# Gate and up of sixteen column tiles of FFN 1 by Strassen, and the SSM preparation rewritten and spread differently

## The chip, the cores and the metric

One NeuronCore of a Trainium2 chip runs the whole kernel in one launch. The metric is the device time of one execution in microseconds (us). The engines are named as in the profile: PE (TensorE, matmuls; PEld is its weight loads), DVE (VectorE), ACT (ScalarE), POOL (GpSimd) and SP (SyncE, which here only issues DMAs). Each engine takes its instructions strictly in the order of the program's queue for it, and waits at an instruction whose operand or buffer is not ready.

## The reference

One decoder layer on x of 512 tokens by 1024 channels, all float32: a half-step SwiGLU, then an SSM and a sliding-window attention side by side, then a second half-step SwiGLU and a last norm.

```python
h = rms_norm(x, ffn1_norm)
x = x + 0.5 * ((silu(h @ w_gate) * (h @ w_up)) @ w_down)      # FFN 1, d_ff = 2816
h = rms_norm(x, mix_norm)
u, q, k, v = split(h @ w_in, [512, 1024, 1152])
y_ssm  = s5_mixer(u, ...)                    # 32 groups of 16 channels, 64 complex states each
y_attn = swa_sink_attention(rope(q), rope(k), v, sinks)       # 8 heads of 64, window 128
x = x + concat(rms_norm(y_ssm), rms_norm(y_attn)) @ w_out
h = rms_norm(x, ffn2_norm)
x = x + 0.5 * swiglu(h, ...)                 # FFN 2, the same shapes
return rms_norm(x, final_norm)

# s5_mixer, from the parameters alone:
lam_bar = exp((A_re + i A_im) * exp(log_dt))
B_bar   = ((lam_bar - 1) / lam) * (B_re + i B_im)
# state[t] = lam_bar * state[t-1] + B_bar @ u[t];  y = Re(C @ state) + D * u, then gelu and a gate
```

## The kernel before

**Matmuls.** Channels lie on the 128 partitions, tokens on the 512 columns. To keep float32 accuracy every operand is split into a high and a low part (`hi`, `lo` of activations, `whi`, `wlo` of weights), and `mm3` (L182 to L184) makes each product of three matmuls: hi x whi, lo x whi, hi x wlo. A weight block comes by DMA into `wraw` (SP's queue), ACT casts it to `whi`, DVE subtracts to get `wlo`; `wraw`, `whi` and `wlo` have three buffers each, so an engine that prepares a block waits until the block three before it has been read.

**FFN.** d_ff is 22 column tiles of 128. A classical tile is two PSUM tiles `gu` (gate and up), each 8 input blocks x 3 matmuls of 512 columns. Tiles come in groups (`FGROUPS`); after each group its activations (`activate`: `g`, `s`, `u`, `a`, then `hi` and `lo`) go into the eight `dn` columns m = 0 to 7 of the down projection, whose results are added to x (`x<-dn,x`). The norm's factor R is not applied to h ahead of the first matmuls but to their results.

**Strassen in FFN 2.** Tiles 6 to 21 of FFN 2 go in eight pairs through `pairs` already: a pair of column tiles and the two halves of tokens and input channels form 2x2 blocks, and gate and up take 7 products each of 4 input blocks x 3 matmuls of 256 columns (PSUM `gua`, `gub`, `guc`). `quarters` prepares the operands on the activation side: h with gain and R applied, sums of its quarters on POOL (`qe`, `q`, `qd`), and their hi and lo parts in `xq`, `xh`, `xr`, `xu`, `xx`. `pair_weights` loads each pair's weights (`wraw`, 512 KB, and two `wb`, 256 KB each, from `wgs2`) and adds four sums on POOL (`s0` to `s3`): `s0` from the two `wb`, `s1` from `s0` and `wraw`. Product n=2 reads `s1`. A product's weights are cast and subtracted two products ahead (`AHEAD`).

**SSM preparation.** `prep_steps` computes from the parameters: the small values (`scr`, 128x32), B_bar and its seven products with powers of lam_bar, one after the other in steps of 256 columns (`chain_b`: 6 POOL operations each, results in `aB`), transposes of these (`tV` on PE, copied to `matV`), the short kernel of the SSM (`qp`, 32 small matmuls with `cbr` and `ncbi`, evaluated to `qs` and written to `dz` in DRAM), the phases `rho`, `ec`, `es` of the state scan by doubling, and C times the powers (`chain_c`: 45 POOL operations of 512 columns, `matC`). The steps are a list; `ffn` takes one from it behind each `gu` tile and each `dn` column of FFN 1, so they spread over all of FFN 1.

**Mixing.** The strings of `ORDER` set in which order the steps of SSM and attention are written: U the projections, K, k and Q, q keys and queries, P the state scan, Y the SSM's output, S and E the scores. The order in which each engine finally gets its instructions comes from a scheduler that works from this program order and the buffers.

## Time and profile before

| | |
|---|---|
| runs | 935.74, 935.38, 925.63 us (median 935.38) |
| profiled execution | span 925.4 us (no time of its own is given; the nearest run is the one of 925.63) |
| granted PE clock, mean | 0.994 |
| PE busy | 907.5 us, 98% |
| DVE, ACT, POOL busy | 624.0, 369.2, 314.9 us |
| FFN 1, mixing, FFN 2 | about 5 to 388, 388 to 559, 559 to 925 us |

A line of a group reads: line of the kernel, engine, operation, result<-operands, shape, how often | busy us in all, mean ns of one | idle us of its engine just before, and what ended that. A line of the timeline reads: start us, duration us, engine, line, operation. PE's ends are modelled, so consecutive matmuls overlap in it.

### The profile page before, as it was taken

To read this page: it belongs to the slowest core of one execution; us is meant where nothing else is said; L and a number is where in the kernel's file an instruction comes from. 1 tells how busy PE (TensorE), PEld (TensorE's weight loads), DVE (VectorE), ACT (ScalarE), POOL (GpSimd) and SP (SyncE) were. 2 spreads that over 40 slices of the span, in tenths; PEclk is the share of its full clock that TensorE was granted. 3 is DMA by queue.
4 is the path that set the end of the run, shared out by engine and by line. 5 is a ranking of instruction groups with operands and counts; after the bars stand their busy time and mean duration, and the time that the engine had idled before them with its cause. 6 is when DMAs were issued, how large, how long until landed. Compare 5 with 4: busy or idle time off the path is not lost.

```text
span 925.4 us, 13303 instructions
## 1 busy us (share of the span) xinstructions
PE 907.5 (98%) x5036; PEld 772.9 (84%) x5036; DVE 624.0 (67%) x1167; ACT 369.2 (40%) x660; POOL 314.9 (34%) x272
## 2 busy tenths in 40 slices
PE   9999999999999999999979999999999999999996
PEld 6887888888888888888868887888899889988995
DVE  7886444474464443958896787697588459855966
ACT  7142233222232322622487433543355335532553
POOL 0009902179950000501231063180553055404502
PEclk9999999999999999999989999999999999999998
DMA  7332423243213321547201122215421442135112
GB/s 244 125 92 53 153 91 103 64 133 121 84 57 112 114 76 56 164 149 186 78 1 46 46 79 104 91 36 157 150 86 35 134 156 87 35 110 180 47 47 91
DMA packets 37503, 91.92 MB, mean 99 GB/s; under 512 B 8032, under 2 KB 10304, under 8 KB 37184
## 3 DMA queue, kind: packets, MB, share of 16 engines
q1 hardware_dynamic: 37008, 90.54, 31.3%
q8 instruction: 39, 0.64, 0.3%
q10 hardware_dynamic: 432, 0.55, 0.2%
q14 instruction: 24, 0.20, 0.1%
HBM read 87.44 MB, written 3.64 MB: 98 GB/s over the span
## 4 chain that ended last, share of the span: by engine, by line
PE 91%; DVE 5%; ACT 2%; issue 1%; DMA 1%; SPq 0%; DVEq 0%; ACTq 0%
PE gu L182 11%; PE gu L183 11%; PE gu L184 11%; PE dn L182 9%; PE dn L183 8%; PE dn L184 8%; PE gua L184 3%; PE gua L183 3%; PE gua L182 3%; PE guc L184 2%; PE guc L182 2%; PE guc L183 2%; PE ow L182 2%; PE ow L183 2%; PE ow L184 2%; PE pt L1037 1%
## 5 line engine op out<-in xcount | busy, mean ns | idle before, releaser
L154 ACT CAST whi<-wraw 128x1024 fp32r<-128x1024 f32 (+4 forms) x134 | 122.6, 921 | 307.6 <-PE gu L183 118.9
L173 DVE TENSOR_TENSOR wlo<-wraw,whi 128x1024 fp32r<-128x1024 f32 (+4 forms) x133 | 155.4, 1173 | 42.6 <-ACT whi L154 42.5
L182 PE MATMUL gu<-hi,whi 128*128 128x512 f32 x448 | 178.9, 402 | 1.5 <-ACT hi L195 1.4
L183 PE MATMUL gu<-lo,whi 128*128 128x512 f32 x448 | 176.7, 395 | 0.1
L184 PE MATMUL gu<-hi,wlo 128*128 128x512 f32 x448 | 176.3, 395 | 0.0
L183 PE MATMUL dn<-lo,whi 128*128 128x512 f32 (+1 forms) x336 | 130.1, 389 | 0.0
L182 PE MATMUL dn<-hi,whi 128*128 128x512 f32 (+1 forms) x336 | 130.1, 392 | 0.0
L184 PE MATMUL dn<-hi,wlo 128*128 128x512 f32 (+1 forms) x336 | 128.9, 389 | 0.0
L182 PEld LDWEIGHTS gu<-hi,whi 128*128 128x128 f32 x448 | 84.4, 189 | 21.8 <-ACT hi L195 2.3
L184 PEld LDWEIGHTS gu<-hi,wlo 128*128 128x128 f32 x448 | 84.3, 188 | 19.7
L183 PEld LDWEIGHTS gu<-lo,whi 128*128 128x128 f32 x448 | 84.5, 189 | 19.2 <-DVE lo L197 1.0
L182 PEld LDWEIGHTS dn<-hi,whi 128*128 128x128 f32 x336 | 63.3, 188 | 14.9 <-ACT whi L154 1.1
L184 PEld LDWEIGHTS dn<-hi,wlo 128*128 128x128 f32 x336 | 63.2, 188 | 14.2
L183 PEld LDWEIGHTS dn<-lo,whi 128*128 128x128 f32 x336 | 63.3, 188 | 13.6
L269 POOL TENSOR_TENSOR sq<-sq 128x512 f32<-128x512 f32 x17 | 25.1, 1476 | 139.9 <-ACT sq L265 137.2
L537 DVE TENSOR_TENSOR wlo<-s,whi 128x512 fp32r<-128x512 f32 x64 | 55.2, 904 | 12.2 <-ACT whi L536 12.0
L502 POOL TENSOR_TENSOR s<-s,wraw 128x512 f32<-128x512 f32 x32 | 50.4, 1576 | 33.9 <-DMA wraw<-wgs 32.9
L502 POOL TENSOR_TENSOR s<-wb 128x512 f32<-128x512 f32 x16 | 23.6, 1474 | 112.3 <-DMA wb<-wgs 91.4
L345 DVE TENSOR_TENSOR u<-gu,R 128x512 f32<-128x512 f32 x28 | 19.2, 685 | 48.2 <-PE gu L184 48.2
L412 DVE SCALAR_TENSOR_TENSOR x<-dn,x 128x512 f32<-128x512 f32 x32 | 21.7, 685 | 42.7 <-PE dn L184 42.7
L536 ACT CAST whi<-s 128x512 fp32r<-128x512 f32 x64 | 36.5, 618 | 30.4 <-issue 9.3
L428 DVE SCALAR_TENSOR_TENSOR x<-dn,x 128x512 f32<-128x512 f32 x24 | 16.5, 690 | 46.2 <-PE dn L184 46.2
(371 smaller groups left out, 2030.1 us busy)
## 6 DMA issues: line engine op xcount, KB each, us to landing
wraw<-wgu SPq DMA_DIRECT2D x54, 512.0 KB, 3.4
wraw<-wd SPq DMA_DIRECT2D x40, 384.0 KB, 3.2
wb<-wgs SPq DMA_DIRECT2D x32, 256.0 KB, 5.2
wraw<-wgs SPq DMA_DIRECT2D x16, 512.0 KB, 3.7
wraw<-wd SPq DMA_DIRECT2D x16, 320.0 KB, 2.9
...
x<-xT SPq DMA_DIRECT2D x8, 256.0 KB, 5.1
...
```

The costliest lines, as they stand in the source:

```text
L154: (e.copy if e is self.nc.scalar else e.tensor_copy)(out, x)
L173: self.eng("lo" + key).tensor_tensor(lo, raw, hi.bitcast(F32), op=ALU.subtract)
L182: mm(out, wh, xh, start=start, stop=False, **kw)
L183: mm(out, wh, xl, start=False, stop=False, **kw)
L184: mm(out, wl, xh, start=False, stop=stop, **kw)
L269: (eng or b.nc.gpsimd).tensor_tensor(self.acc, self.acc, sq, op=ALU.add)
L345: nc.vector.tensor_tensor(u, pu, self.R, op=ALU.mult)
L412: nc.vector.scalar_tensor_tensor(self.x[m], ps, 0.5, self.x[m], op0=ALU.mult, op1=ALU.add)
L428: self.nc.vector.scalar_tensor_tensor(self.x[m], ps, 0.5, self.x[m], op0=ALU.mult, op1=ALU.add)
L502: add = lambda o, x, y: nc.gpsimd.tensor_tensor(o, x, y, op=ALU.add)
L536: self.chained("A", lambda: A.copy(hi[:, c], w))
L537: self.chained("V", lambda: V.tensor_tensor(lo[:, c], w, hi[:, c].bitcast(F32), op=ALU.subtract))
```

## The change

FFN 1 gets what FFN 2 has: its groups become (0,6), (6,12), (12,18), (18,22), and tiles 6 to 21 go through `pairs(1, ...)`. `quarters(1)` prepares the operands during tiles 4 and 5 and the first down; its buffers are taken from tiles that the SSM preparation used (`rce`, `u4`, `big`) and from the pool of 512-column tiles, which grows from 43 to 49.

The SSM preparation is rewritten. A table of the powers of lam_bar (`pw`, `ppw`) replaces the step-by-step chains: `b_powers` makes `aB` with 24 operations of 512 columns, half on POOL and half on DVE, and `c_powers` makes `matC` with 24, likewise. The exponential of `er`, the B_bar factor and the copies go from DVE to POOL. Everything up to `qp` and `dz` is done by the end of the first down (`early`); `rho`, `ec`, `es`, the doublings and `matC` are done in the last down and in the mixing stage (`late`, the new `B` entries of `ORDER`). The loads of `s_prm`, `sB`, `cbr`, `cbi` and `sD` go from SP's queue to ACT's.

```diff
-FGROUPS = {1: ((0, 6), (6, 12), (12, 17), (17, 22)), 2: ((0, 6), (6, 12), (12, 18), (18, 22))}
+FGROUPS = {1: ((0, 6), (6, 12), (12, 18), (18, 22)), 2: ((0, 6), (6, 12), (12, 18), (18, 22))}
-ORDER = ("R0 U0 U1 R1 u0 u1 l0 U2 U3 u2 u3 l1 K0 P0 K1 L0 k0 P1 C0 L1 t0 C1 Y0 C2 C3 q0 q2 Q0 q1 Q2 q3 Y1 S0 "
+ORDER = ("R0 U0 B3 U1 B1 R1 u0 u1 l0 U2 B1 U3 B1 u2 u3 l1 K0 B1 P0 K1 L0 k0 B2 P1 C0 B2 L1 t0 B2 C1 Y0 C2 C3 q0 q2 Q0 q1 Q2 q3 Y1 S0 "
...
-        self.m2p = ctx.enter_context(tc.tile_pool(name="m2p", bufs=43))
+        self.m2p = ctx.enter_context(tc.tile_pool(name="m2p", bufs=49))
...
+    def ffn1(self):
+        xg, wgu, wd = self.xg, self.d["wgu1"], self.d["wd1"]
+        early, self.late = self.prep_steps()
+        prep = self.quarters(1)
+        take = lambda q, n: [q.pop(0) for _ in range(n)]
+        slots = [take(early, n) for n in (1, 1, 2, 2, 2, 3, 2, 0)]
+        scale = prep.pop(0)
+        slots += [take(prep, 1), take(prep, 1), take(early, 4) + take(prep, 2), take(early, 4) + take(prep, 1),
+                  take(early, 1) + take(prep, 1), [], [], take(early, 1) + take(prep, 1)]
...
+        scale()
+        self.down(wd, 0, NCL, acts, background)
+        for f0, f1 in FGROUPS[1][1:]:
+            acts = self.pairs(1, range((f0 - NCL) // 2, (f1 - NCL) // 2))
+            if f1 < NF:
+                self.down(wd, f0, f1, acts, lambda m: None)
+        self.prenorm(self.g_mix)
...
-        def chain_b(s):
+        def b_powers(r, q4):
             def f():
...
+                e = (G, V)[r]
+                qs = slice(q4 * 4, q4 * 4 + 4)
...
+                t = [S.m2(name="tB").rearrange("p (q c s) -> p q c s", q=4, s=T) for _ in range(2)]
+                tt(t[0], x[r], y[0], ALU.mult, e)
+                tt(t[1], x[1 - r], y[1], ALU.mult, e)
+                tt(aB[:, r, qs], t[0], t[1], (ALU.subtract, ALU.add)[r], e)
             return f
...
-            nc.sync.dma_start(cr, d["sCbd"][:, 0])
-            nc.sync.dma_start(ci, d["sCbd"][:, 1])
-            nc.sync.dma_start(dd, d["sD"])
+            for t, src in ((cr, d["sCbd"][:, 0]), (ci, d["sCbd"][:, 1]), (dd, d["sD"])):
+                nc.scalar.dma_start(t, src)
...
+        def c_powers(g8, e):
             def f():
...
+                tt(t[0], x[0], y[0], ALU.mult, e)
+                tt(t[1], x[1], y[1], ALU.mult, e)
+                tt(S.matC[:, gs], t[0], t[1], ALU.add, e)
             return f
...
+        for g8 in range(8):
+            late.append(c_powers(g8, (G, V)[g8 % 2]))
```

At the start of FFN 1, ACT's queue held before: `hi` of the last two x tiles, the first `whi` of tile 1, the eight squares `sq`, six more `whi`; now it holds the eight squares and the load of `sB` ahead of the first `whi` of tile 1. Ahead of the activation of tile 5, DVE's queue now holds all twelve DVE operations of `b_powers` (`tB`, `aB`). Three places in rows:

PE, at the first `qp` matmul. Before, it stood in the second group's `gu` tiles:

```order
L183 MATMUL gu<-lo,whi 128x512
L184 MATMUL gu<-hi,wlo 128x512
L854 MATMUL qp<-cbr,aB 128x32
L182 MATMUL gu<-hi,whi 128x512
L183 MATMUL gu<-lo,whi 128x512
```

Now it stands in the first down, between the last matmul of column m=5 and the first of m=6:

```order
L182 MATMUL dn<-hi,whi 128x512
L183 MATMUL dn<-lo,whi 128x512
L184 MATMUL dn<-hi,wlo 128x512
L909 MATMUL qp<-cbr,aB 128x32
L182 MATMUL dn<-hi,whi 128x512
```

ACT at the same place, now (`xr`, `xm`, `xu` are parts of the quarter-operands, made from POOL's sums `q`, `qe`, `qd`; `whi` of L559 is the first product of the first pair, of L154 a down column's):

```order
L478 ACTIVATE xr<-qe 128x512 x2
L475 CAST xm<-h 128x256 x2
L154 CAST whi<-wraw 128x768
L475 CAST xm<-h 128x256 x2
L475 CAST xu<-qd 128x512
L475 CAST xm<-h 128x256 x2
L478 ACTIVATE xr<-q_1015 128x512
L475 CAST xm<-h 128x256 x2
L559 CAST whi<-wraw 128x512 x2
L903 DMA cbr<-sCbd 128x512
L903 DMA cbi<-sCbd 128x512
```

The load of `cbr` has moved behind casts that wait for POOL and for a weight buffer. Before, SP issued it among the weight loads of the second group:

```order
L171 DMA wraw<-wgu 128x1024 x12
L171 DMA wraw<-wd 128x768
L846 DMA cbr<-sCbd 128x512
L847 DMA cbi<-sCbd 128x512
L848 DMA sD<-sD 128x512
L171 DMA wraw<-wd 128x768 x5
L872 DMA dz<-qs 16x8x256
L869 DMA dz<-zero 16x7x256 x2
L872 DMA dz<-qs 16x8x256
```

SP now, from the loads of the first down on (`wb` of the first row of two are gate's of the first pair, of the second up's):

```order
L171 DMA wraw<-wd 128x768 x8
L521 DMA wraw<-wgs 128x1024 x3
L524 DMA wb<-wgs 128x512 x2
L927 DMA dz<-qs 16x8x256
L924 DMA dz<-zero 16x7x256 x2
L927 DMA dz<-qs 16x8x256
L524 DMA wb<-wgs 128x512 x2
L521 DMA wraw<-wgs 128x1024 x2
```

The four `dz` transfers, which stood among the last weight loads of a down, now stand between the weights of gate and up of one pair. DVE in the mixing stage, at the end of the state scan (`wr`, `ro`, `S`), before; `kL` belongs to the keys, and `ra`, `rb`, `q` rotate the queries:

```order
L1172 TENSOR_TENSOR ro_3825<-wi,ec 128x512
L1184 TENSOR_TENSOR S<-ro_3822,ro_3823 64x4x63 x4
L1184 TENSOR_TENSOR S<-ro_3824,ro_3825 64x4x63 x4
L173 TENSOR_TENSOR wlo<-wraw,whi 128x1024
L1063 TENSOR_TENSOR kL<-tk,kH 64x512 x2
L1142 TENSOR_TENSOR ra<-q,cst 128x128
```

and now:

```order
L1220 TENSOR_TENSOR ro_4896<-wi,ec 128x512
L173 TENSOR_TENSOR wlo<-wraw,whi 128x1024
L663 TENSOR_TENSOR tC<-X_4560,s_pwr 128x512
L663 TENSOR_TENSOR tC<-Y,s_pwi 128x512
L1232 TENSOR_TENSOR S<-ro_4893,ro_4894 64x4x63 x4
L1111 TENSOR_TENSOR kL<-tk,kH 64x512
L1232 TENSOR_TENSOR S<-ro_4895,ro_4896 64x4x63 x4
L663 TENSOR_TENSOR matC<-tC 128x512
L663 TENSOR_TENSOR tC<-X_4560,s_pwr 128x512
L663 TENSOR_TENSOR tC<-Y,s_pwi 128x512
L1111 TENSOR_TENSOR kL<-tk,kH 64x512
L663 TENSOR_TENSOR matC<-tC 128x512
```

Six operations of `c_powers` have come between the state scan and the rotation of the queries; three more stand further up in the scan.

More of the change, by code (lines that the diff above doesn't have):

```diff
@@ L277, in consts @@
         nc.scalar.dma_start(self.gains, self.d["gains"])
+        self.prm = self.cp.tile([P, 3 * NG], F32, name="s_prm")
+        nc.scalar.dma_start(self.prm, self.d["sprm"])
         self.ident = self.cst[:, 0:128]
@@ new lines, in ffn1, with background, after @@
+    def ffn1(self):
[7 more added lines that the diff above has]
+                  take(early, 1) + take(prep, 1), [], [], take(early, 1) + take(prep, 1)]
+        assert not early and not prep
+        def background(_=None):
+            for f in slots.pop(0):
+                f()
+        hooks = {(1, 1): self.first_norm, (2, 1): self.norm_bcast}
+        acts, pend = [], []
+        for f in range(NCL):
+            if f == 0:
+                pend.append(self.first_pair(1, wgu, xg))
+                continue
+            pair = []
+            for gu in range(2):
+                wh, wl = self.weight(wgu[f, gu].rearrange("p k m -> p (k m)"), 1024)
+                ps = self.ps("gu")
+                for k in range(KT):
+                    self.mm3(ps, wh[:, k * P:(k + 1) * P], wl[:, k * P:(k + 1) * P], xg[k][0], xg[k][1],
+                             k == 0, k == KT - 1)
+                pair.append(ps)
+                hooks.get((f, gu), background)()
+            pend.append(pair)
+            while pend and f >= max(hooks)[0]:
+                acts.append(self.activate(*pend.pop(0)))
+        scale()
[5 more added lines that the diff above has]
+        self.prenorm(self.g_mix)
+        def after(m):
+            self.prenorm_tile(m)
+            if m < 3:
+                self.late.pop(0)()
+        self.down(wd, f0, f1, acts, after)
@@ new lines, in homes @@
+        def homes():
+            r = [cp.tile([P, 1024], F32R, name="xr", tag="rce", bufs=3) for _ in range(3)]
+            u = [cp.tile([P, 1024], F32R, name="xu", tag="u4", bufs=2) for _ in range(2)]
+            home("n2", r[:2])
+            home("t1", (r[2], cp.tile([P, 1024], F32R, name="xx", tag="xx")))
+            home("t3", u)
+            if i == 1:
+                for n in ("b11", "b21"):
+                    self.xq[n] = [[self.m2(F32R, "xm") for _ in range(2)] for _ in range(2)]
+            else:
+                half = [cp.tile([P, 2, 1024], F32R, name="xh", tag="half", bufs=2) for _ in range(2)]
+                for n, t in zip(("b11", "b21"), half):
+                    home(n, (t[:, 0], t[:, 1]))
+                big()
@@ L874, in prep_steps @@
         S.dz = dz
-        S.rho, S.ec, S.es = (cp.tile([P, NP, NCH], F32, name=n, tag="rce", bufs=3) for n in ("rho", "ec", "es"))
+        step(S.drain)
         def square(c, s):
@@ L895, in square @@
             return co, so
-        @step
+        @later
         def _():
+            S.rho, S.ec, S.es = (cp.tile([P, NP, NCH], F32, name=n, tag="rce", bufs=3) for n in ("rho", "ec", "es"))
             e2, e4, e8 = (self.tiny(NP, f"e{n}") for n in (2, 4, 8))
@@ L929, in prep_steps @@
         while n < NCH:
-            steps.append(double(n))
+            late.append(double(n))
             n *= 2
-        @step
+        @later
         def _():
-            S.drain()
             S.matC = big("matC").rearrange("p (g s c) -> p g s c", g=NG, s=T)
@@ L1119, in mixing @@
                "M": self.attn_rstd, "W": lambda m: out_half(0, m), "X": lambda m: out_half(1, m), "w": ssm_add,
-               "x": attn_add}
+               "x": attn_add, "B": lambda n: [self.late.pop(0)() for _ in range(n)]}
         for step in ORDER.split():
```

345 lines of the change are left out of this document (159 added, 186 removed).

## The prediction

> **What bounds the kernel now.** I read the page's busy time and its chain first, then the start-to-start spacing of matmuls in the timeline, then the waits at the places where the change puts new instructions.
>
> ```profile
> span 925.4 us, 13303 instructions
> PE 907.5 (98%) x5036; PEld 772.9 (84%) x5036; DVE 624.0 (67%) x1167; ACT 369.2 (40%) x660; POOL 314.9 (34%) x272
> ...
> PE 91%; DVE 5%; ACT 2%; issue 1%; DMA 1%; SPq 0%; DVEq 0%; ACTq 0%
> ...
> PE pt L1329 <- ACT pr L1308: 4.7, 1, 4.7
> PE gu L182 <- ACT hi L195: 1.4, 2, 0.9
> ```
>
> PE (TensorE) carries 91% of the chain and is almost never late: the longest waits in the list of PE's waits are one of 4.7 us in attention and two, 1.4 us together, at the very start. In FFN 1 behind its start PE waits for nobody. So a matmul saved there is time saved, and a wait put there is time lost, one for one. The 5% of DVE in the chain lie in the mixing stage, which the change also touches.
>
> PE's busy time is modelled (a 512-column matmul shows 0.40 us and the next starts 0.23 us later), so I price matmuls by the distance of their starts:
>
> ```profile
> 245.02 0.40 PE L182 MATMUL gu<-hi,whi 128*128 128x512 f32 x1
> ...
> 250.62 0.40 PE L182 MATMUL gu<-hi,whi 128*128 128x512 f32 x1
> ...
> 662.36 0.28 PE L182 MATMUL gua<-xq,whi 128*128 128x256 f32 x1
> ...
> 665.24 0.28 PE L182 MATMUL gub<-xq,whi 128*128 128x256 f32 x1
> ...
> 668.12 0.28 PE L182 MATMUL gua<-xr,whi 128*128 128x256 f32 x1
> ```
>
> The first two rows are 24 matmuls of 512 columns apart: 5.60/24 = 0.2333 us. The other three are FFN 2's Strassen products, 24 matmuls of 256 columns apart: 2.88/24 = 0.120 us.
>
> **What it saves.** Two column tiles, gate and up, take 4 x 24 = 96 matmuls classically: 22.40 us. By Strassen they take 7 products x 2 x 12 = 168 small ones: 20.16 us. That is 2.24 us a pair, and for 8 pairs **-17.9 us**. The downs keep their number of matmuls (22 tiles for each of 8 down columns either way, the last two groups 6 and 4 instead of 5 and 5), and so do the transposes and the `qp` matmuls.
>
> Inside the new stage I expect what FFN 2 shows: POOL's 8 additions a pair are 12.5 us by their rows (1.474 to 1.618 us, quoted below) beside 20.16 us of PE, and FFN 2's products run without a gap. So the steady state costs nothing; the price is in how the stage is entered, and in where the rewritten preparation lands. Five places:
>
> **1. The start, +2 us.** In the new order ScalarE does the eight squares of the norm ahead of the `whi` cast of tile 1.
>
> ```profile
> 12.55 1.41 ACT L195 ACTIVATE hi<-x,gains 128x512 fp32r<-128x512 f32 x2 [0.21 <-DMA x<-xT]
> 14.55 1.05 ACT L154 CAST whi<-wraw 128x1024 fp32r<-128x1024 f32 x1 [0.59 <-DMA wraw<-wgu]
> 15.51 4.27 ACT L265 ACTIVATE sq<-x 128x512 f32<-128x512 f32 x8
> ...
> 17.86 0.40 PE L184 MATMUL gu<-hi,wlo 128*128 128x512 f32 x1
> 18.09 0.40 PE L182 MATMUL gu<-hi,whi 128*128 128x512 f32 x1
> ```
>
> Tile 0 ends on PE at 18.09 (the last row is the 49th `gu` matmul, tile 1's first). The `hi` of the first row end at 12.55 + 1.41 = 13.96. Squares directly behind them last until 18.23, plus 1.05 for the cast: PE waits to 19.3, 1.2 us. The first matmuls then alternate between gate and up, so the second cast (20.3) costs 0.5 more, and `wlo` on DVE stands behind five square additions. Bounds: 1.2 us, and 4 us if each of these waits is paid in full. I take 2.
>
> **2. The first down, +5 us.** Twelve DVE operations of `b_powers` (512 columns) now stand ahead of the activation of tiles 4 and 5, and the first down cannot end without those.
>
> ```profile
> L345 DVE TENSOR_TENSOR u<-gu,R 128x512 f32<-128x512 f32 x28 | 19.2, 685 | 48.2 <-PE gu L184 48.2
> ```
>
> No row shows these multiplications with spread operands; the nearest is this two-input one of the same size: 12 x 0.685 = 8.2 us, and two copies of `matV`, by the same row, add 1.4. PE has matmuls of the other four tiles for the first three down columns as cover (36 x 0.2333 = 8.4 us) and 32 transposes, but the activations themselves already used most of it. Bounds: 0 (the cover reaches) and 8.2; I take 5.
>
> **3. `qp` waits for its operand, +8 us.** `cbr` used to be loaded from SP's queue long before. Now ScalarE issues it, behind a cast `whi` of the first pair. That cast reuses the buffer that the sixth down column (m=5) reads, so it waits for PE to end that column; and on PE the first `qp` matmul stands directly behind that column. From the column's end to `qp` there are at least two casts and the landing:
>
> ```profile
> L536 ACT CAST whi<-s 128x512 fp32r<-128x512 f32 x64 | 36.5, 618 | 30.4 <-issue 9.3 <-PE gua L183 8.6 <-PE gub L183 7.5
> ...
> cbr<-sCbd SPq DMA_DIRECT2D x1, 256.0 KB, 3.4
> ...
> L445 POOL TENSOR_TENSOR h<-h,R 128x512 f32<-128x512 f32 x4 | 6.6, 1676 | 26.9 <-ACT h L444 26.9
> ...
> L471 POOL TENSOR_TENSOR qe<-h 128x256 f32<-128x256 f32 x4 | 3.9, 998 | 0.0
> ...
> L472 POOL TENSOR_TENSOR q<-h,qe 128x256 f32<-128x256 f32 x4 | 3.6, 888 | 0.0
> ```
>
> Lower end: 2 x 0.62 + 3.4 = 4.6 us, whatever else happens. Upper end: ScalarE also has to work off the split quarter-operands, and these wait for POOL: four `h` at 1.68 and fourteen sums of 256 columns at about 1.0 make 20.7 us from the moment tile 5 is activated, then some 2.5 us of casts and 3.4 of landing, 26.6. PE meanwhile has three whole down columns and the last sixth of three others, 63 x 0.2333 = 14.7, and 16 transposes, about 2: it waits 10. I take 8, nearer the upper end, because every part of that sum has a row.
>
> **4. The first pair's up weights, +4 us.** On SP the four `dz` transfers stand ahead of up's two `wb`, and `dz` waits for `qs`, which needs the last `qp`, the matmul just ahead of the first product. So `wb` is issued when the products begin.
>
> ```profile
> wb<-wgs SPq DMA_DIRECT2D x32, 256.0 KB, 5.2
> ...
> L502 POOL TENSOR_TENSOR s<-wb 128x512 f32<-128x512 f32 x16 | 23.6, 1474 | 112.3 <-DMA wb<-wgs 91.4 <-PE guc L184 19.9 <-DVE wlo L173 1.0
> ...
> L502 POOL TENSOR_TENSOR s<-s,wraw 128x512 f32<-128x512 f32 x32 | 50.4, 1576 | 33.9 <-DMA wraw<-wgs 32.9
> ...
> L537 DVE TENSOR_TENSOR wlo<-s,whi 128x512 fp32r<-128x512 f32 x64 | 55.2, 904 | 12.2 <-ACT whi L536 12.0
> ...
> 9.45 0.33 SPq L700 DMA_DIRECT2D s_prm<-sprm  x1
> ```
>
> Product n=2 of up reads s1: `qs` 0.69, four issues of 0.33, landing 5.2, two additions 1.47 + 1.58, cast 0.62 and `wlo` 0.90 make 11.8 us. Products 0 and 1 and gate's half of product 2 cover 60 x 0.120 = 7.2. That leaves 4.6; with a landing as quick as that of the other weights in these rows (3.4, `cbr`) 2.8. I take 4.
>
> **5. The mixing stage, +6 us.** Here DVE is the engine to ask, because `matC`, half of it now on DVE and half on POOL, is computed beside the state scan.
>
> ```profile
> 420.00:430.00 10.00, 10.00 (x122) 9.34 (x121) 10.00 (x26) 3.33 (x9) 0.00 (x0) 1.00 0.74 190
> 430.00:440.00 10.00, 10.00 (x47) 7.71 (x45) 9.83 (x18) 1.76 (x2) 2.72 (x3) 1.00 0.65 177
> 440.00:450.00 10.00, 10.00 (x88) 8.65 (x88) 9.83 (x17) 3.78 (x7) 0.42 (x1) 1.00 0.01 5
> ...
> 429.86 1.69 DVE L1184 TENSOR_TENSOR S<-ro,ro 64x252 f32<-64x252 f32 x4
> ...
> 434.03 3.83 DVE L1184 TENSOR_TENSOR S<-ro,ro 64x252 f32<-64x252 f32 x4
> ...
> 434.52 2.63 POOL L173 TENSOR_TENSOR wlo<-wraw,whi 128x1024 fp32r<-128x1024 f32 x1 [42.43 <-ACT whi L154]
> ...
> 451.20 0.69 DVE L1063 TENSOR_TENSOR kL<-tk,kH 64x512 fp32r<-64x512 f32 x1 [1.24 <-ACT kH L1062]
> ...
> 455.09 0.45 PE tq L1077 x4
> 455.57 0.59 ACT qT L1086
> 456.18 0.70 DVE qT L1087
> ```
>
> The first three rows give, for each stretch, its length and then the busy time of PE, PEld, DVE, ACT and POOL: DVE 29.66 of 30 us. Behind 455 the chain runs through DVE. Nine of the twelve new DVE operations stand in this stretch, at 0.6 us from start to start (the spacing of the scan's 512-column rows) 5.4 us; free are 1.2 us before the second `kL` and 0.5 before `tq`. So 3.7 us at least reach the chain unless PE and ScalarE absorb them (then 0). And the two `S` rows show the other price: the same four operations took 1.69 us with POOL idle and 3.83 with POOL at a two-input subtraction beside them. POOL has 12 `matC` operations here where it had almost nothing. If all twelve, at about 1.5 us, slow DVE in that measure, DVE gives up 18 x (1 - 1.69/3.83) = 10 us more. Bounds 0 and 14; I take 6.
>
> **Costed at nothing:** the small operations of the new preparation on POOL, and the 42 wide ones of `chain_b` and 45 of `chain_c` that it loses (POOL is in no step of the chain); `rho`, `ec`, `es` and their doublings, now behind the last down (POOL's row of the page is empty or nearly so in the slices before and behind, 268 to 373 and 393 to 430 us); the loads of `s_prm` and `sB`, moved from SP to ScalarE, 0.33 us each to issue by the row above, inside the bounds of place 1. Without that cover the doublings would hold up the first state scan by their own length, some 10 us; no row says that they do.
>
> The sum: -17.9 + 2 + 5 + 8 + 4 + 6 = **+7 us**, put on the profiled execution (span 925.4 us; the run nearest to it took 925.63): 932.6. The other two runs of before took 935.4 and 935.7, so the program itself spreads by 10 us; I forecast 933 for the median and leave the spread to the range. 2% (some 18.6 us) is about what a measurement of this kernel can tell from no change.
>
> **The rivals.**
>
> *The saving survives.* The waits overlap (a PE that is late at the first down finds POOL, ScalarE and `cbr` less late), and the mixing stage absorbs its share. With only the floors, 1.2 + 4.6 + 2.8 and 0 elsewhere, it is -17.9 + 8.6 = -9 us: 916 us, and not below 908 even with no wait at all. For it: PE's waits in before are tiny although its order is just as crowded. Against it: the floors of 3 and 4 follow from places in in-order queues.
>
> *Slower.* POOL's `matC` work drags DVE through the state scan and the scores start late: the upper end of place 5, +14, and with the others at their upper ends (4 + 8.2 + 10 + 4.6) +23 us: 948. It decides from about 13 us in mixing. For it: the `S` rows. Against it: PE is itself busy with `pt` matmuls up to 455, so that DVE has until then to catch up.
>
> *The small matmuls do not run at 0.120 us.* Every small matmul needs its own weight load, and there are 576 more of them.
>
> ```profile
> L182 PEld LDWEIGHTS gu<-hi,whi 128*128 128x128 f32 x448 | 84.4, 189 | 21.8 <-ACT hi L195 2.3
> ...
> L182 PEld LDWEIGHTS gua<-xr,whi 128*128 128x128 f32 x128 | 24.6, 192 | 0.0
> ```
>
> If loads stood in line with the streams, 96 x (0.233 + 0.189) = 40.5 us would become 168 x (0.120 + 0.192) = 52.4, +95 us over 8 pairs: 1020 us. But a spacing of 0.120 is shorter than the load of 0.192 itself, so loads overlap here already; I give it 1%. The Trainium skill's page "TensorE: Matmul & The Clock Gate", section "The mechanism" of Part 3, says that a weight load overlaps matmuls in flight only when its row group differs; all loads here use all 128 rows, so by that rule this rival would be the result. The spacing of 0.120 us in FFN 2 disagrees with it.
>
> **How the numbers follow.** Forecast (no change that can be told, 919 to 945): 0.69. Saving survives: 0.18. Slower: 0.12. Small matmuls slow: 0.01. Against the median the 2% lie at 916.7 and 954.1, against the profiled run at 907 and 944, and a comparison of fresh runs may fall on either; so about half of the saving case counts as faster (0.09, and 0.01 from the forecast's lower edge), and three quarters of the slow case as slower (0.09, with 0.01 from the edge and 0.01 from the small matmuls). The rest, 0.79, is no change. The range cuts the lower part of the saving case and the top of the slow one: 914 to 950, which also takes in the spread of the runs.
>
> **What would show it.** Right: FFN 1's products at 0.120 us from start to start without gaps behind the first pair; among PE's waits a `qp` on the transfer of `cbr` (5 to 10 us), a `gua` on `wlo` or `whi` of product 2 (3 to 5), `gu` on `whi` near 18 us, `dn` on `lo` in the first down; DVE solid from about 415 on, and `tq` or `kL` late. Wrong: no wait at `qp`, since then the ScalarE order does not bind PE as I read it; products with gaps in every pair, since then POOL or DVE can't feed FFN 1; or a mixing stage that is shorter than before.

## The result: 4.4% slower, and the profile after

The changed kernel takes 969.49 us (median; 968.58 to 971.83), the kernel before beside it 931.11; the ratio is 1.0437, 95% interval [1.0379, 1.0496]. The profiled execution has a span of 967.2 us against 925.4: **41.8 us more**, where the sum of the prediction gave 7 more. Runs of the kernel before come near 926 us (mean granted clock 0.992 to 0.995) or near 935 us (0.982 to 0.984), a few near 956; the profiled one is of the first kind, and all spans below are compared with it.

The head of the page and its chain, of the changed kernel:

```profile
span 967.2 us, 14918 instructions
...
PE 910.1 (94%) x5612; PEld 802.1 (83%) x5612; DVE 736.0 (76%) x1272; ACT 423.2 (44%) x820; POOL 393.3 (41%) x369
...
PE 70%; DVE 18%; issue 4%; ACT 3%; POOL 2%; DMA 2%; SPq 0%; DVEq 0%; POOLq 0%; ACTq 0%
```

PE's share of the chain falls from 91% to 70%, DVE's rises from 5% to 18%: PE now waits, mostly for VectorE. The list of PE's waits names where (us in all, times, longest):

```profile
PE gua L182 <- ACT fa L586: 7.2, 1, 7.2
PE qp L909 <- DMA cbr<-sCbd: 5.5, 1, 5.5
PE tq L1125 <- DVE q L1193: 4.7, 1, 4.7
PE prb L252 <- DVE dg L248: 4.7, 1, 4.7
...
PE tk L1105 <- DVE kt L1193: 4.4, 1, 4.4
PE pu L183 <- DVE lo L197: 3.6, 2, 2.9
PE dn L182 <- ACT hi L203: 3.2, 2, 2.8
PE dn L184 <- DVE wlo L173: 1.8, 2, 1.1
```

`gua` is the first matmul of product 2 of the first pair, `qp` and `dn` are in the first down; `pu`, `prb`, `tk` and `tq` are all in the mixing stage (`prb` broadcasts the norm's factor, `tk` and `tq` transpose keys and queries). Of the waits of 2 us and more only one (4.7 us on `pr`, here 4.4) was there before.

The next table cuts the profiled executions by the first matmul of each stage, in us. "First pairs" is gate and up of tiles 6 to 11, where the pairs' own matmuls need 60.5 (before: classical, 67.2, and `tV` and most `qp` matmuls among them). The first down's own matmuls take 33.5. "Mixing" runs from the first `pu` to the first `ow`.

| | tiles 0 to 5 | first down | first pairs | mixing | span |
|---|---|---|---|---|---|
| before | 70.5 | 34.1 | 75.6 | 121.3 | 925.4 |
| after | 73.0 | 62.3 | 71.4 | 147.5 | 967.2 |
| cbr early | 72.3 | 54.1 | 72.4 | 150.4 | 962.3 |
| cbr early, dz late | 71.5 | 55.1 | 68.2 | 150.1 | 957.9 |
| no late work | 72.0 | 60.7 | 71.6 | 125.0 | 942.6 |
| preparation without Strassen | 71.9 | 55.8 | 68.6 | 150.3 | 970.1 |
| doublings in third down | 71.6 | 65.7 | 71.3 | 137.4 | 959.4 |
| matC on GpSimd | 73.6 | 62.1 | 71.8 | 156.3 (see 6) | 980.6 |
| matC on VectorE | 71.7 | 63.6 | 72.2 | 149.5 | 969.4 |

**The saving is there.** Products of the second group of pairs, 48 matmuls apart:

```profile
245.76 0.28 PE L182 MATMUL gua<-xm,whi 128*128 128x256 f32 x1
...
251.45 0.28 PE L182 MATMUL gua<-xr,whi 128*128 128x256 f32 x1
```

5.69/48 = 0.1185 us each. Three undisturbed pairs take 60.2 us and two take 40.2, where the same tiles done classically (in "preparation without Strassen") take 66.9 and 44.6. That is 6.7 and 4.4 us, so 17.8 for eight pairs.

**What I had not priced: PE's clock halves behind a wait.** In the first down, behind the wait for `hi` (start, duration, operation):

```profile
91.96 0.40 PE L184 MATMUL dn<-hi,wlo 128*128 128x512 f32 x1
95.15 1.55 PE L182 MATMUL dn<-hi,whi 128*128 128x512 f32 x3 [2.79 <-ACT hi L203]
...
97.35 0.63 PE L183 MATMUL dn<-lo,whi 128*128 128x512 f32 x1
97.78 0.63 PE L184 MATMUL dn<-hi,wlo 128*128 128x512 f32 x1
...
98.90 0.39 PE L182 MATMUL dn<-hi,whi 128*128 128x512 f32 x1
```

Starts are 0.43 us apart; from 98.90 on they are 0.23 again. Cut at the right places, the table of stretches shows the granted clock (the number behind the five engines' busy times) at 0.51:

```profile
91.80:95.20 3.40, 0.61 (x4) 0.17 (x2) 2.61 (x6) 1.35 (x3) 0.00 (x0) 1.00 0.00 0
95.20:98.60 3.40, 3.40 (x8) 2.65 (x9) 3.40 (x4) 3.40 (x6) 2.80 (x2) 0.51 0.00 0
...
119.10:125.90 6.80, 5.22 (x13) 4.23 (x14) 5.79 (x12) 1.12 (x3) 0.94 (x2) 0.51 0.78 268
...
149.80:156.60 6.80, 3.26 (x15) 3.26 (x16) 3.55 (x6) 3.53 (x8) 5.41 (x4) 0.51 0.10 17
```

The stretches last 3.4 or 6.8 us, once 10.2. The trace of the changed kernel has ten of them ahead of the kernel's end, some 51 us in all; that of before has one of 6.8, behind its one long wait. By these spacings a stretch costs about half of the part of it in which PE works: in the last row PE works only 3.26 of 6.8 us, since the stretch begins while PE still waits. One of the ten, from 132.8 us on, has no wait of PE directly in front of it; there 26 narrow `qp` matmuls run in 3 us. So a wait is not the only thing that brings the slow clock.

**And what happened in mixing.** VectorE's small operations of the norm chain, in the kernel before and then after, with GpSimd's doublings beside them:

```profile
396.52 0.16 DVE L218 SCALAR_TENSOR_TENSOR rs_y<-rs_u,rs_y 128x4 f32<-128x4 f32 x1
396.71 0.16 DVE L214 TENSOR_TENSOR rs_t<-rs_y 128x4 f32<-128x4 f32 x1
```

```profile
419.78 0.97 DVE L218 SCALAR_TENSOR_TENSOR rs_y<-rs_u,rs_y 128x4 f32<-128x4 f32 x1
420.79 0.97 DVE L214 TENSOR_TENSOR rs_t<-rs_y 128x4 f32<-128x4 f32 x1
421.79 0.97 DVE L216 SCALAR_TENSOR_TENSOR rs_u<-rs_t,rs_v 128x4 f32<-128x4 f32 x1
...
419.69 1.05 POOL L663 TENSOR_TENSOR tE<-ec,q_co 128x512 f32<-128x512 f32 x1
420.69 1.05 POOL L663 TENSOR_TENSOR tE<-es,q_so 128x512 f32<-128x512 f32 x1
421.70 1.05 POOL L663 TENSOR_TENSOR tE<-ec,q_so 128x512 f32<-128x512 f32 x1
```

An operation on four columns lasts 0.97 us instead of 0.16, and ends in step with the GpSimd operation beside it. From here on I call this **taking turns**.

### The profile page after: what moved, and what is told of

It reads as the page before. It is cut to its first block, busy times and chain, and to the rows that moved or that the text cites. A ratio compares the mean times of both kernels' runs of the same rounds, so it can differ in the third digit from the quotient of the medians.

```text
span 967.2 us, 14918 instructions
## 1 busy us (share of the span) xinstructions
PE 910.1 (94%) x5612; PEld 802.1 (83%) x5612; DVE 736.0 (76%) x1272; ACT 423.2 (44%) x820; POOL 393.3 (41%) x369
## 4 chain that ended last, share of the span: by engine, by line
PE 70%; DVE 18%; issue 4%; ACT 3%; POOL 2%; DMA 2%; SPq 0%; DVEq 0%; POOLq 0%; ACTq 0%
PE dn L182 7%; PE dn L184 7%; PE dn L183 7%; PE gua L184 6%; PE gua L182 6%; PE gua L183 6%; PE guc L184 3%; PE guc L183 3%; PE guc L182 3%; PE gu L182 3%; PE gu L184 3%; PE gu L183 3%; DVE wlo L173 2%; PE ow L182 2%; PE ow L183 2%
## 5 line engine op out<-in xcount | busy, mean ns | idle before, releaser
L154 ACT CAST whi<-wraw 128x768 fp32r<-128x768 f32 (+4 forms) x102 | 88.7, 879 | 160.5 <-PE dn L183 54.8
L560 DVE TENSOR_TENSOR wlo<-s,whi 128x512 fp32r<-128x512 f32 x128 | 110.3, 904 | 29.0 <-ACT whi L559 28.7
L526 POOL TENSOR_TENSOR s<-s,wraw 128x512 f32<-128x512 f32 x64 | 99.7, 1557 | 59.9 <-DMA wraw<-wgs 32.7
L173 DVE TENSOR_TENSOR wlo<-wraw,whi 128x768 fp32r<-128x768 f32 (+4 forms) x101 | 114.9, 1145 | 10.1 <-ACT whi L154 10.1
L559 ACT CAST whi<-s 128x512 fp32r<-128x512 f32 x128 | 73.0, 618 | 63.8 <-PE gua L183 18.5
L182 PE MATMUL gu<-hi,whi 128*128 128x512 f32 x192 | 76.7, 406 | 2.4 <-ACT whi L154 1.6
L184 PE MATMUL gu<-hi,wlo 128*128 128x512 f32 x192 | 76.1, 399 | 1.4 <-DVE wlo L173 1.4
L183 PE MATMUL gu<-lo,whi 128*128 128x512 f32 x192 | 76.7, 400 | 0.1
L560 DVE TENSOR_TENSOR wlo<-wraw,whi 128x512 fp32r<-128x512 f32 x64 | 61.0, 985 | 0.0
L559 ACT CAST whi<-wraw 128x512 fp32r<-128x512 f32 x64 | 36.0, 614 | 40.3 <-PE dn L183 39.3
L526 POOL TENSOR_TENSOR s<-wraw,wb 128x512 f32<-128x512 f32 x32 | 52.5, 1641 | 0.0
L182 PEld LDWEIGHTS gu<-hi,whi 128*128 128x128 f32 x192 | 36.8, 192 | 12.6 <-ACT whi L154 3.5
```

Source lines behind the costliest of these rows:

```text
L154: (e.copy if e is self.nc.scalar else e.tensor_copy)(out, x)
L173: self.eng("lo" + key).tensor_tensor(lo, raw, hi.bitcast(F32), op=ALU.subtract)
L182: mm(out, wh, xh, start=start, stop=False, **kw)
L183: mm(out, wh, xl, start=False, stop=False, **kw)
L184: mm(out, wl, xh, start=False, stop=stop, **kw)
L526: add = lambda o, x, y: nc.gpsimd.tensor_tensor(o, x, y, op=ALU.add)
```

## The experiments

Theory: the waits, each with its halved clock, make FFN 1 slower; in mixing the late work on VectorE and GpSimd makes `prb`, `tk` and `tq` late. Rivals: VectorE's load as such, or the pairs themselves.

**1. `cbr`, `cbi` and `sD` loaded at the start.**

```diff
@@ step of sB @@
+            for t, src in ((cr, d["sCbd"][:, 0]), (ci, d["sCbd"][:, 1]), (dd, d["sD"])):
+                nc.scalar.dma_start(t, src)
@@ step of qp @@
-            for t, src in ((cr, d["sCbd"][:, 0]), (ci, d["sCbd"][:, 1]), (dd, d["sD"])):
-                nc.scalar.dma_start(t, src)
```

> The changed kernel (969.0 us), with cbr, cbi and sD loaded together with sB, a hundred microseconds before qp needs them, and ncbi made then. Theory (a wait of PE costs its own length, and then half of the time in which the granted clock is halved behind it): the wait of 5.5 us and 3.4 of the 6.8 us of slow clock behind it go: 960 us. Rival 1 (only the wait counts): 963.5. Rival 2 (PE only waits elsewhere instead, for the same ScalarE casts behind POOL's sums): 967 to 970.

Measured: 964.11 us, ratio 1.0366 [1.0241, 1.0491]. The wait of `qp` is gone and the first down is 8.2 us shorter, more than the 5.5 us of the wait: its slow stretch went too (5.3 us of it lay behind the wait's end). The total gained 4.9 in span, because mixing took 2.9 more.

**2. The same, and `dz` written in the second down, behind the first pair's weights.**

```diff
-            for h in range(2):
-                nc.sync.dma_start(dz[h, :, T:]...
+        def write_dz():          # called in the second down, m = 0
+            for h in range(2):
+                nc.sync.dma_start(dz[h, :, T:]...
```

> As before, and the four dz transfers stand behind the weight loads of the third pair on SP, so that up's wb of the first pair are not held up. Theory: the wait of 7.2 us in front of product 2 goes too, with 3.4 of the slow clock behind it: 949 us. Rival 1 (only the waits): 956. Rival 2 (the first pair waits for POOL's sums of weights instead): 958 or more.

Measured: 959.79 us, ratio 1.032 [1.0195, 1.0444]. PE's waits among the first pairs fall from 7.2 us to these:

```profile
PE gua L184 <- DVE wlo L560: 2.9, 2, 2.3
PE gua L182 <- ACT fa L586: 1.3, 1, 1.3
```

The group of the first pairs takes 68.2 us, 4.2 less. So `dz` ahead of the weights was most of that wait, but 4.2 us of waits stay, and a slow stretch of 6.8 us, which costs some 3. The theory's 949 was too hopeful.

**3. No late work.** `rho`, `ec`, `es` and `matC` are filled with a constant.

```diff
+        late[:] = [blank] + [lambda: None] * 15     # blank: memset of rho, ec, es, matC to 0.5
```

> The changed kernel without the late preparation: rho, ec, es and matC are filled by memsets on POOL in the last down, their computation is left out. Between the first pu and the first ow matmul it is 121.4 us before and 147.6 after. Theory (the late operations on POOL and DVE hold up the norm's chain and the state scan): that stage returns to 118 to 124 us and the total to 941 to 947. Rival (the stage is long because FFN 1 ends on ScalarE and DVE late, or because of the clock alone): it stays above 135, total 957 or more.

Measured: 948.77 us (944.41 profiled), ratio 1.0201 [1.0036, 1.0366]; mixing 125.0 us; no wait of `prb` or `tk`, and `tq` waits 0.6 us as it did before. The late work costs 22.5 of mixing's 26.2 us more.

**4. The new preparation, gate and up classical in all tiles.**

```diff
-            acts = self.pairs(1, range((f0 - NCL) // 2, (f1 - NCL) // 2))
+            # per tile: two gu tiles of 8 x mm3, then activate, as in tiles 1 to 5
-        prep = self.quarters(1)
+        prep = [lambda: None] * 8
```

> The rewritten and moved preparation alone: gate and up of all 22 tiles of FFN 1 classical as before, in the groups of the change, no quarter-operands. Theory (most of the loss is the preparation's, and Strassen itself saves its 17.9 us less 10 to 12 at its entry): the start, the first down without POOL's sums (qp then waits 0 to 3 us) and the mixing stage remain: 927 + 3 + 8 + 26 = 964 us. Rival (the loss is in Strassen's entry, and the preparation alone costs little): 930 to 945.

Measured: 971.48 us, ratio 1.0445 [1.0319, 1.0571]. That is only 2 us from the changed kernel, whose own runs spread by 3, and most of it lies in mixing, which the edit does not touch; the stages of FFN 1 add up to within 1 us of the changed kernel's (397.1 and 396.5 us). So Strassen nets next to nothing of its 17.8: the rest pays for the first pair's wait with its slow clock and for `cbr`, which is later behind the quarter sums (the first down takes 55.8 us here). The rewritten preparation alone is as slow as the whole change.

**5. The doublings of `rho`, `ec`, `es` in the third down.**

```diff
-                self.down(wd, f0, f1, acts, lambda m: None)
+                self.down(wd, f0, f1, acts, lambda m: self.late.pop(0)() if f0 == 12 and m < 7 else None)
@@ after(m) of the last down @@
-            if m < 3:
-                self.late.pop(0)()
```

> The changed kernel, but rho, ec, es and their doublings on GpSimd are done in the third down of FFN 1 and no longer beside the norm chain behind the last down (in buffers of their own). In the changed kernel the mixing stage (first pu matmul to first ow matmul) took 147.5 us, before 121.3, without all late work 125.0. Theory, small VectorE operations take turns with GpSimd's: the norm chain is back at 0.2 us an operation, the waits of pu and prb (3.6 and 4.7 us) and most of the halved clock around them go, stage 135 to 139, run about 958 to 961. Rival 1, the whole of VectorE's and GpSimd's load in the stage decides, wherever it stands: the matC operations still press on tk and tq, stage 141 to 146. Rival 2, the third down pays for it: its 33.5 us grow by 3 or more.

Measured: 961.45 us, ratio 1.0339 [1.0215, 1.0463]; mixing 137.4, the third down 33.5 as before. Mixing is 10.1 us shorter, the theory's size is right and the third down pays nothing, but `prb` still waits (6.6 us): `matC` has moved up beside the norm chain and takes turns with it. The first down, with six tile buffers fewer, grew by 3.4.

**6 and 7. `matC` on one engine.**

```diff
-            late.append(c_powers(g8, (G, V)[g8 % 2]))
+            late.append(c_powers(g8, G))        # 6; in 7: V
```

> The changed kernel with all 24 operations of matC on GpSimd (12 of them were on VectorE). Theory A, VectorE's load decides in the state scan: it loses 12 operations of 1.4 to 1.8 us, the waits of tk and tq (4.4 and 4.7 us) go, mixing stage 132 to 138 us against 147.5. Theory B, the two engines taking turns decides: GpSimd holds VectorE up for twice as long, stage 147 to 157, tk and tq as late as now or later.

> The changed kernel with all 24 operations of matC on VectorE, none on GpSimd. Theory A, VectorE's load decides: 12 more operations of 0.7 us at least, mixing stage 152 to 160 us against 147.5. Theory B, the taking of turns decides: with GpSimd idle in the scan each VectorE operation of 512 columns is back at 0.6 to 0.7 us instead of 1.4 to 1.8, which saves more than the 8 us that are added, stage 138 to 145.

Measured: 981.88 us on GpSimd (mixing 156.3), 971.46 on VectorE (149.5). The first stage is as theory B said (of its two waits `tk` is later, `tq` is not), the second lies between the two. Some 6 us of the 156.3 come from a stretch of halved clock at the stage's end. Experiments 12 and 13, without this edit, have the same stretch, so it is probably not the edit's, though no run here shows what brings it on:

```profile
545.90:558.90 13.00, 13.00 (x66) 13.00 (x65) 5.22 (x12) 6.87 (x21) 0.00 (x0) 0.51 0.01 1
```

Without it the stage takes 150, no less than with `matC` divided. The groups of VectorE from 440 to 500 us say why, first of the changed kernel, then with all of `matC` on VectorE:

```profile
L663 DVE TENSOR_TENSOR matC<-tC 128x512 f32<-128x512 f32 x4 | 6.3, 1565 | 0.0
...
L663 DVE TENSOR_TENSOR tC<-Y,s_pwi 128x512 f32<-128x512 f32 x4 | 3.6, 909 | 0.0
L663 DVE TENSOR_TENSOR tC<-X,s_pwr 128x512 f32<-128x512 f32 x4 | 3.5, 865 | 0.0
```

```profile
L663 DVE TENSOR_TENSOR tC<-X,s_pwr 128x512 f32<-128x512 f32 x8 | 5.4, 681 | 0.0
L663 DVE TENSOR_TENSOR tC<-Y,s_pwi 128x512 f32<-128x512 f32 x8 | 5.4, 680 | 0.0
L663 DVE TENSOR_TENSOR matC<-tC 128x512 f32<-128x512 f32 x8 | 5.3, 683 | 0.0
```

Twelve operations beside GpSimd took VectorE 13.4 us; twenty-four without it 16.1. The half that GpSimd took over bought VectorE 2.7 us. Which wait it falls on changes with the order (on VectorE alone `tk` waits only 0.6 us, but `tq` 11.5), the sum hardly does.

**8 and 9. The b powers on one engine** (8 with edit 1, 9 with edits 1 and 2).

```diff
-                e = (G, V)[r]
+                e = G        # 8; in 9: V
```

> The loads of cbr, cbi and sD early (as in the run with 964.1 us, whose first down took 54.1 us), and all 24 operations of the b powers on GpSimd, so that none stands on VectorE ahead of the activation of tiles 4 and 5. Theory, those VectorE operations make the first down late: it shrinks to 44 to 48 us, run 954 to 958. Rival, GpSimd is the engine that is late there: 12 more operations of about 1.5 us put the quarter sums and aB back by 18 us, the first down stays at 54 or grows to 65, run 964 to 975.

> The run with cbr, cbi, sD loaded early and dz written late (960 us; its first down took 55.1 us, where matmuls alone need 41.9), with all 24 operations of the b powers on VectorE. Theory, what makes the first down late are the two engines taking turns (beside GpSimd the operation tB took 1.55 to 1.78 us on VectorE, alone 0.68): 24 at 0.6 to 0.7 are no more than 12 at up to 1.8, and GpSimd is free for the quarter sums; first down 46 to 51 us, run 951 to 956. Rival, VectorE's load: the activation of tiles 4 and 5 comes later still, first down 56 to 64.

Measured: 964.82 us with a first down of 57.4, and 959.82 with 57.9; against 54.1 and 55.1 with the powers divided, so here dividing the work gains some 3 us. Both rivals were right: on GpSimd the transposes wait (`tV` on `aB`, 7.0 us), on VectorE `dn` waits for `hi` (5.0 us). Neither engine takes the powers alone without a loss in the first down.

**10 and 11. The powers left out, the quarters left out** (both with edit 1).

```diff
-                steps.append(b_powers(r, q4))
+                steps.append(lambda r=r, q4=q4: G.memset(aB[:, r, q4 * 4:q4 * 4 + 4], 0.5))    # 10
@@ 11: as experiment 4 @@
```

> The run with the early loads (964 us, first down 54.1 us, of which 43.8 are matmuls: 33.5 of its own and 10.3 of tV and qp), with the 24 operations of the b powers left out and aB filled with a constant by eight memsets on GpSimd; transposes, qp and everything behind stay. Theory, the powers ahead of tiles 4 and 5 make the first down wait: waits of dn (7.1 us) and the slow clock behind them go, first down 44 to 47 us. Rival, the quarter-operands of the first pair do it: 51 to 55.

> The same run with early loads, but gate and up of all tiles classical, so that no quarter-operands are prepared; the b powers as they are. Theory, the powers make the first down wait: it stays at 52 to 55 us. Rival, the quarter-operands do: 44 to 47.

Measured: first down 43.9 us without the powers, 54.0 without the quarters (whole: 950.12 and 968.15, one run each). The 43.9 are the matmuls and nothing else: 33.5 of the down and 10.3 of `tV` and `qp`, which before lay in the second group (75.6 - 67.2 = 8.4) and the second down (35.4 - 33.5 = 1.9). From 70 to 140 us PE's only listed wait without the powers is the first pair's:

```profile
PE gua L182 <- ACT fa L586: 7.0, 1, 7.0
```

So with `cbr` loaded early the powers in front of tiles 4 and 5 cost the first down its other 10 us, the quarters nothing.

**12 and 13. A wait put into the kernel before.** Multiplications by 1 on GpSimd delay the activation of tile 16, the last of the third group, at a place where PE waits for nothing.

```diff
         nc.vector.tensor_tensor(a, s, u, op=ALU.mult)
+        for _ in range(hold):                       # tile 16 alone: 5 (12), or 12 (13)
+            nc.gpsimd.tensor_scalar(a, a, 1.0, None, op0=ALU.mult)
```

> The kernel before, with five multiplications by 1 on GpSimd put into the activation of tile 16 of FFN 1, where GpSimd has nothing else to do and where matmuls run without a gap: the third down (27.9 us) then waits for it once, some 4 us. Theory, a wait of PE halves its granted clock behind it: matmuls of 512 columns follow at 0.43 us for 3.4 or 6.8 us, the down takes the wait and 1.7 to 3.4 us more. Rival, the low clock in the changed kernel has another cause (what PE computes there, the load of the other engines): matmuls at 0.233 throughout, the down longer by the wait alone.

> The same with twelve multiplications, a wait of some 10 to 13 us. Theory: as with five, 0.43 us from start to start for 3.4 to 10 us behind the wait; if the length of the wait sets the length of the slow stretch, a longer one than with five. Rival: 0.233 throughout.

The third down took 32.1 and 43.5 us instead of 27.9 (whole: 939.43 and 951.13, one run each). With five, the stretches before and behind the wait, and PE's rows there:

```profile
283.60:287.00 3.40, 1.09 (x5) 0.62 (x4) 0.55 (x1) 0.62 (x1) 2.08 (x2) 1.00 0.00 0
287.00:290.40 3.40, 3.40 (x10) 2.57 (x9) 2.33 (x5) 2.18 (x3) 0.00 (x0) 0.57 0.00 0
290.40:293.80 3.40, 3.40 (x15) 2.70 (x15) 1.90 (x3) 0.00 (x0) 0.00 (x0) 0.92 0.73 199
...
286.47 0.96 PE L182 MATMUL dn<-hi,whi 128*128 128x512 f32 x3 [2.31 <-ACT hi L203]
...
287.98 0.63 PE L183 MATMUL dn<-lo,whi 128*128 128x512 f32 x1
288.40 0.63 PE L184 MATMUL dn<-hi,wlo 128*128 128x512 f32 x1
```

2.3 us of wait cost 4.2. This is the same stage with the same matmuls, so the halved clock comes from the wait and not from what the changed kernel computes. With twelve:

```profile
287.80:301.50 13.70, 4.09 (x10) 3.23 (x11) 2.25 (x4) 2.35 (x4) 8.49 (x6) 0.51 0.00 0
...
297.41 1.65 PE L182 MATMUL dn<-hi,whi 128*128 128x512 f32 x3 [13.31 <-ACT hi L203]
```

13.3 us cost 15.6, 2.3 on top: the clock falls while PE still waits and comes back some 4 us after it goes on. So in these two runs the surcharge is some 2 us a wait, short or long: the slow stretch grows with the wait, but not the work that falls into it.

Both whole times hold 10 us more, which need not be the edit's: a stretch of 20.5 us at 0.51 from the end of mixing on, which the profile of before does not show.

```profile
505.40:525.90 20.50, 20.50 (x94) 19.62 (x94) 7.73 (x19) 8.43 (x25) 0.00 (x0) 0.51 0.00 1
```

The stretch begins among the attention's transposes and narrow matmuls, 13 us ahead of `ow`, as it does in experiment 6. Half of its length, 10 us, is as much as the spread from 926 to 935 us; that it is the cause of that spread is likely and not shown.

**14 and 15. GpSimd kept busy beside the norm chain of before**, by twelve operations that nobody reads.

```diff
+        junk = self.m2(name="junk")
+        for _ in range(12):
+            G.tensor_tensor(junk, self.x[0], self.x[1], op=ALU.mult)          # 14
+            G.tensor_scalar(junk, self.x[0], 2.0, None, op0=ALU.mult)         # 15, in its place
```

> The kernel before, with twelve independent two-input multiplications (128x512) on GpSimd at the beginning of the mixing stage, beside the norm chain that runs on VectorE from 394.7 to 398.2 us in operations of 0.16 us. Theory, small VectorE operations take turns with GpSimd's: each of them takes about as long as the GpSimd operation beside it (1.0 to 1.7 us), the broadcast prb is 7 to 12 us late, the mixing stage grows from 121.3 to 126 to 133. Rival, in the changed kernel these operations are long because of VectorE's own load: they stay at 0.16 to 0.25 us, the stage at 121 to 123.

> The kernel before with twelve one-input multiplications by a constant (128x512) on GpSimd beside the norm chain, in the place of two-input ones (with these the chain of small VectorE operations took 0.16 and 1.14 us in turn, prb came 8 us late, stage 131.0 us). If only GpSimd's two-input operations make VectorE take turns: all at 0.16 us, stage 121 to 123. If any GpSimd operation does: every other one at the length of a GpSimd operation again, stage 127 to 132.

With two inputs mixing takes 131.0 us (121.3 before), with one input 121.1. The chain on VectorE beside two-input operations:

```profile
420.08 0.16 DVE L218 SCALAR_TENSOR_TENSOR rs_y<-rs_u,rs_y 128x4 f32<-128x4 f32 x1
420.27 1.15 DVE L214 TENSOR_TENSOR rs_t<-rs_y 128x4 f32<-128x4 f32 x1
421.46 0.17 DVE L216 SCALAR_TENSOR_TENSOR rs_u<-rs_t,rs_v 128x4 f32<-128x4 f32 x1
421.66 1.14 DVE L218 SCALAR_TENSOR_TENSOR rs_y<-rs_u,rs_y 128x4 f32<-128x4 f32 x1
```

and beside one-input ones, with GpSimd's own row:

```profile
394.67 13.57 POOL L991 TENSOR_SCALAR junk<-x 128x512 f32<-128x512 f32 x8
...
396.59 0.16 DVE L218 SCALAR_TENSOR_TENSOR rs_y<-rs_u,rs_y 128x4 f32<-128x4 f32 x1
396.79 0.16 DVE L214 TENSOR_TENSOR rs_t<-rs_y 128x4 f32<-128x4 f32 x1
```

Taking turns is shown as a cause by itself, in a kernel without any of the change: with two-input GpSimd operations every other small operation waits some 1 us. With one-input ones the chain's small operations stay short but for a few (0.55 the longest). The Trainium skill, page "SBUF — State Buffer", section "SBUF: two separate sides", says that VectorE operations with two SBUF inputs and GpSimd operations take a shared pair of ports as a lock for the whole instruction. The two-input rows agree with that; the one-input rows, where such a GpSimd operation also reads SBUF, do not.

The whole of the two-input run, 955.50 us, holds another 20 us that were not meant. In the first down, where the old preparation keeps GpSimd busy without a pause, one VectorE operation that lasts about 1 us elsewhere took

```profile
87.44 19.31 DVE L173 TENSOR_TENSOR wlo<-wraw,whi 128x768 fp32r<-128x768 f32 x1
```

and `dn` waited 17.7 us for it. No other profile of this case has such a row.

**16. All late work ahead of mixing**: edits 1, 2 and 5, and `matC` in the last down.

```diff
@@ after(m) of the last down @@
+            if m < 5:
+                for _ in range(1 + (m > 0)):
+                    self.late.pop(0)()
```

> The changed kernel with all of the late work taken out of the mixing stage and the two early waits removed: cbr, cbi and sD loaded early, dz written behind the first pair's weights, rho, ec, es and the doublings on GpSimd in the third down, matC in the last down (half GpSimd, half VectorE). The changed kernel takes 969, with the two early edits alone 960. Theory, late work beside the norm chain and the scan costs the stage: mixing from 150 back to 125 to 130 us, run 936 to 942, still behind the kernel before. Rival 1, the last down pays in its place (22 us with VectorE busy in 16.6 of them, 8.4 us more to do): it grows by 4 to 10, run 942 to 948. Rival 2, with the waits gone the Strassen saving shows: 920 to 930.

Measured: 961.97 us, ratio 1.0357 [1.0284, 1.0429]; mixing 148.5, the last down 23.5 (22.3 before the edit). The theory fell. `matC` does not fit into the last down: with half on each engine its operations take 1.6 to 1.8 us on VectorE and last until 419, 26 us past the first `pu` matmul, and much that mixing needs first stands behind them. The first `pu` matmuls wait 10.1 us for their `wlo` and 8.4 for `lo`, in the place of `prb`, `tk` and `tq`.

**17 and 18. The best of it**: edits 1, 2 and 5 with `matC` on VectorE in mixing (17), and also the b powers on VectorE (18).

> The same two early edits, with rho, ec, es and the doublings in the third down (stage 137.4 us when done alone) and matC all on VectorE in the mixing stage. Theory, taking turns: VectorE without GpSimd beside it does 24 operations at 0.6 to 0.7 us instead of 12 at 1.4 to 1.8, the stage takes 128 to 134 us, run 940 to 946. Rival, VectorE's load: the query's transpose tq waits 10 us or more for it, as it did with matC on VectorE and the doublings beside it (11.5 us), stage 138 to 146, run 950 to 956.

> All of these together: early loads, late dz, the doublings in the third down, the b powers and matC on VectorE alone. If both theories of taking turns hold: 932 to 940 us, within 2% of the kernel before. If neither: 955 or more.

Measured: 949.35 us, ratio 1.0212 [1.012, 1.0304], and 950.57, ratio 1.0234 [1.0163, 1.0306]. Mixing takes 135.5 and 135.6 us, between theory and rival; `tq` waits 3.9 us instead of 10 or more. This is 20 us better than the change and still about 2% behind the kernel before. Of 17's span over before (21.6 us) the stages hold: 13.3 in the first down behind the moved matmuls, 7.2 in the first pairs, 14.2 in mixing, some 5 elsewhere, less 17.8 of saving. No version beats the kernel before. Moving the powers clear of the first down was not tried; by experiment 10 it is worth up to 10 us.

## Why the prediction was wrong

| step | predicted | measured |
|---|---|---|
| saving of eight pairs | -17.9 | -17.8 |
| 1, start | +2 | +2.5 |
| 2 and 3, first down (less 10.3 moved matmuls) | +5 and +8 | +17.9 |
| 4, first pairs | +4 | +10.9 |
| 5, mixing | +6 | +26.2 |
| FFN 2 | 0 | +2.5 |

The measured steps add up to 42.2, the spans differ by 41.8. Most of what I named came: `qp` on `cbr`, `gua` behind `dz` (on `fa`, not on `wlo` or `whi`), `dn` late in the first down (on `hi` and `wlo`, not on `lo`), VectorE full and `tq` late. Not named were the waits of `pu`, `prb` and `tk` in mixing, 12.7 us together. The saving is right to 0.1 us, and the rival of slow small matmuls is out. What failed were the sizes of the steps, a cost of the waits that I had left out (the slow clock), and a term that I had put at nothing (the doublings). Of FFN 2's 2.5 us two waits of PE make 2.1 (1.4 on a `wlo`, 0.7 on `tailw`); why they came is open.

**Places 2 and 3** were sized as waits alone. The first down waits 11.0 us (5.5 for `qp`, 5.5 for `hi`, `wlo` and x), below the 13 that I took; of 13.6 us of slow stretches some 12 lie behind the waits, and half of those, 6 us, come on top. That my 8 for place 3 meets the 8.2 us of experiment 1 is luck: the wait was 5.5, and the other 2.7 are the slow clock. Place 2 was too low: 10 us by experiment 10, against 5 and an upper end of 8.2. The twelve VectorE operations took 9.1 us, near the 8.2 of my row, so their price was right; what I had wrong is how much of it PE's other matmuls hide, as in experiment 1 PE still waits 7.1 us in the first down, and the slow clock comes on top.

**Place 4.** The wait is 7.2 us, by itself above the 4.6 that I had as the upper end; the slow clock behind it adds 1.7, and short stalls in the second and third pair some 2. The chain was the one I described, but longer: `qs` begins at 140.41, as the last `qp` ends, the first `wb` is issued at 143.56, and the first sum waits for the second until 149.77,

```profile
149.77 1.26 POOL L526 TENSOR_TENSOR s<-wb 128x512 f32<-128x512 f32 x1 [18.42 <-DMA wb<-wgs]
...
153.34 0.58 PE L182 MATMUL gua<-xr,whi 128*128 128x256 f32 x1 [7.19 <-ACT fa L586]
```

6.2 us where I took 5.2, with 2.4 us instead of 1.3 for the four `dz` ahead of it; in all 12.9 us from `qs` to the waiting matmul, where I had 11.8. And the cover was shorter. PE waits by name for `fa`, the copy that frees gate's `gua`; on ScalarE it stands behind the cast of up's sum. So gate's half of product 2, which I had counted as cover, waits too: 48 matmuls of 0.120 are 5.8 us, not the 7.2 of 60.

The row that could have warned me of the clock was in the profile of before, behind the one wait of 4.7 us that I quoted:

```profile
473.00:480.00 7.00, 5.77 (x25) 5.27 (x26) 4.97 (x32) 7.00 (x35) 0.00 (x0) 0.53 0.00 0
```

The Trainium skill's page "TensorE: Matmul & The Clock Gate", Part 1, "The HAM clock gate (the "warmup" mystery)", gives the idle window behind which the clock halves, and the busy one that brings it back, as about 3.4 us. The length of the stretches agrees; the start does not quite, since 2.31 us of wait (experiment 12) and 2.79 us (first down) were enough. Nor does the length of the wait alone decide: in experiment 11 a wait of 2.79 us at the same place in the first down had no slow stretch behind it.

**Place 5** is the large miss: 26.2 against 6, above my upper end of 14. I priced the `matC` operations by the `S` rows (1.69 and 3.83 us), which is the right mechanism: taking turns. Two things were left out. I counted the doublings as free because GpSimd was idle there; moving them away gave 10.1 us (experiment 5), because the norm chain on VectorE beside them is one of small operations, and most of them wait for the GpSimd operation beside them. And GpSimd's half of `matC` saves VectorE almost nothing, as twelve operations at up to 1.6 us are nearly twenty-four at 0.68 (experiments 6 and 7). So the rival "slower" had the right engine and a price that was too low by half, and its chance of 0.12 was too small: I let PE's `pt` matmuls absorb delays which they do not reach, since `prb` and `tk` stand ahead of them or among them.
